# Two more up pairs in two by two form, and the first half's down rows added to x1 in DRAM

## The chip, the cores and the metric

The kernel runs on one core of one Trainium2 chip. The metric is the device time of one execution in microseconds (us). Before the change it is 693.52 us, the median of three runs (693.3 to 694.15). One further execution was taken with the hardware profiler; all rows quoted here come from it.

The engines are called as the profile calls them: PE (TensorE, matrix products; PEld is its loading of weights), DVE (VectorE), ACT (ScalarE), POOL (GpSimd) and SP (SyncE, which here only issues transfers). POOL also issues transfers, among them those that add to what already lies in DRAM.

## What is computed

A residual block for 512 tokens with 1024 channels: a normed input projection, a short convolution beside an attention, a gated merge, then a channel mixer. The change is in the channel mixer:

```python
h = rms_norm(x, norm_ffn_g[l])
up = causal_dwconv(h @ w_up[l], conv_ffn_w[l])
a, b = jnp.split(up, 2, axis=-1)
x = x + (jax.nn.silu(a) * b) @ w_down[l]
...
return rms_norm(x, norm_f_g)
```

`FFN_HIDDEN` is 2816, so `a` and `b` have 22 blocks of 128 channels each. The convolution has three taps along the tokens.

## The kernel before, in words

**Products in three parts.** Every matrix product is made of three in a rounded type: high part of the weights by high part of the data, low by high, high by low. So each weight tile that arrives (`raw_...`, on SP's queue, five buffers) is split by ACT into a high part (`wh_...`, line 267) and by DVE into a low part (`wl_...`, line 271). There are two buffers of each, so a split starts when PE has done with the tile two before.

**Two by two form.** Part of the products are computed on two by two blocks of quarters with seven products where eight would be usual. Such a product needs sums of weight quarters (made in DRAM ahead of time), sums of data quarters (made once by DVE), and sums of the results in PSUM (made by DVE). Weights in this form come as two chunks for each step: `P` (three plain quarters, from `wst`) and `F` (four sums, from `sums`).

**Sums of weights.** `todo` is a list of transfers, six for each group of weights: SP copies a part from `wst` (line 140), POOL adds another part onto it (line 143), and so on in turn, each waiting for the one before. One of the list is issued with each `tick()`, and `split()` ticks as the kernel goes along the stream of weights.

**The channel mixer's order.** Pairs j = 0 to 21 (one block of `a`, one of `b`) are made in two halves: pairs 0 to 11, then a pass over the down products with what they gave (`down`, 12 steps; its matmuls are `dn`), then pairs 12 to 21 and a second pass of 8 steps, and a plain rest and the last norm. In a plain pair each of the two blocks (`block`, matmuls `p_up`) takes 48 matmuls of 128 by 256; pairs 3 and 7 (`UPS`) are in two by two form (`up_pair`, matmuls `us`, then five sums on DVE, lines 1087 to 1092) with 84. They need the forms of x1 (sums of its quarters), which lie in the tile `xf`. After pair 7 the place of these forms is used again: its lower half takes x1 itself, reloaded from its copy `x1d` in DRAM by two transfers of POOL (line 1097), and its upper half is space for temporaries (`fz`).

**Behind each block** DVE multiplies with the norm's factor (`up`, line 1110), ACT and DVE apply the three taps (lines 603, 604, 607; output `fu`, three buffers), ACT applies silu to `a`, and POOL multiplies `a` by `b` (line 1123 for even pairs, 1130 for odd ones). For each two pairs DVE then forms quarter sums (lines 1140 to 1145), and ACT and DVE split the results into `gh` and `gl` (lines 1149, 1150), the data of the down products. Up to pair 7 the multiply works in place in PSUM, from pair 8 on it writes into `fz`.

**Down rows.** The output's first six row blocks are done as three rows i = 0, 1, 2 of two blocks in two by two form, the first half also row 3. The 8 PSUM banks are two sets, `X` and `Y`. When the products of a row are complete, `combine` puts seven sums on DVE and a copy on ACT into the list `later`, which `split()` works off beside the splits; they add the row to x1 in `xg`. Row 2 of the first half is `HELD`: its four banks (set Y) are not read out but stay open until the second pass goes on adding to them. So the second half's up blocks turn in the four banks of set X alone.

**One row read early.** For the end of the kernel, a piece of x1's last row is split into `gh` and `gl` (lines 1304, 1305). These need nothing but the reloaded x1.

Of the kernel before, what the change touches and what calls it, by code (L numbers as in the profile page):

```python
# [13 lines left out]
P = 128  # L14
D = 1024
S = 512
# [37 lines left out]
HELD = 2  # L54
GS = 2
NFF = len(STEPS[0]) + len(STEPS[1])
UPS = (3, 7)
# [7 lines left out]
def block_kernel(ctx, tc, xT, vecs, wv, win, wmix, wo, wup, wst, wdp, outT):  # L65
# [56 lines left out]
    ngate = len(groups)  # L122
    groups += [[NUP + 2 * j, NUP + 2 * j + 1] for j in range(len(UPS))]
    nup = len(groups)
    groups += [list(range(n, min(n + 2, NFF - 1))) for n in range(0, NFF - 1, 2)] + [[NFF - 1]]
# [28 lines left out]
    for i0, i1 in ((0, ngate), (ngate, len(groups))):  # L154
        for i in range(i0, i1, 4):
            todo += [op for ops in zip(*(group(x) for x in range(i, min(i + 4, i1)))) for op in ops]
# [83 lines left out]

    def split(hl=None):
# [6 lines left out]
        if k >= gs0 and (nm[0] in "imwu" or nm[0] == "F" and int(nm[1:]) % 2):  # L248
            tick()
            if nm[0] in "m":  # L250
                tick()
# [916 lines left out]
    def combine(ph, i, banks, ids):  # L1168

        m1, m2 = x1[:, 2 * i, :], x1[:, 2 * i + 1, :]  # L1170
        p23, p45, p16, p7 = banks[0], banks[1], banks[2], banks[3][:, th[0]]
        t = {}

        def z1():
            t["z"] = fz(f"cz{ph}{i}")
            nc.scalar.activation(t["z"][:, th[0]], p16[:, th[0]], AF.Copy)
            nc.vector.tensor_add(t["z"][:, th[1]], p16[:, th[1]], t["z"][:, th[0]])

        def a1():
            nc.vector.tensor_add(m1, p23, m1)  # L1180

        def u3():
            t["u"] = fz(f"cu{ph}{i}")[:, : 2 * P]
            nc.vector.tensor_add(t["u"], p7, t["z"][:, th[1]])
            nc.vector.tensor_add(m1[:, th[1]], p45[:, th[1]], m1[:, th[1]])

        def a2():
            nc.vector.tensor_sub(m2, m2, p45)

        def a3():  # L1190
            nc.vector.tensor_add(m1, m1, t["z"])

        def a4():
            m2h = m2.rearrange(halves_of, h=2)
            nc.vector.tensor_sub(m2h, m2h, t["u"].unsqueeze(1).to_broadcast([P, 2, 2 * P]))

        for f, us, x in ((z1, 0.42, 2), (a1, 0.7, 0), (u3, 0.85, 3), (a2, 0.7, 1), (a3, 0.7, None), (a4, 0.7, None)):
            later.append((0, us, () if x is None else ids if x == 3 else (ids[x],), f))
        if ph == 1:
            for m in (2 * i, 2 * i + 1):  # L1200
                later.append((0, 0.8, (), lambda m=m: final_square(m)))

# [18 lines left out]
    def down(ph, n0):  # L1221
# [13 lines left out]
        for n, (name, prods) in enumerate(todo):  # L1235
# [5 lines left out]
            for cs, i, g, b, h in prods:  # L1241
                if i not in open_:
# [235 lines left out]
```

## Time and profile before

| stage | from, us | to, us | PE busy | DVE busy | DMA share |
|---|---|---|---|---|---|
| projection, attention | 0.00 | 182.00 | 180.88 | 133.72 | 0.57, then 0.72 |
| gates and merge | 182.00 | 294.70 | 112.66 | 87.77 | 0.81 |
| output projection | 294.70 | 338.20 | 43.50 | 34.22 | 0.76 |
| pairs 0 to 11 | 338.20 | 466.60 | 128.40 | 111.98 | 0.71 |
| first down pass | 466.60 | 523.70 | 57.10 | 42.78 | 0.84 |
| pairs 12 to 21 | 523.70 | 632.50 | 108.80 | 77.95 | 0.51 |
| second down pass | 632.50 | 668.20 | 35.70 | 29.16 | 0.55 |
| rest and last norm | 668.20 | 691.40 | 17.26 | 16.48 | 0.26 |

The profiled execution itself took 693.39 us; its span, from the first to the last instruction, is 691.4 us. The table is read off windows of busy time: in a stage where PE's busy time is as long as the stage, PE had something to do throughout, and the time of the other engines lies beside it.

### The profile page before, as it was taken

What the parts mean: (1) busy time and instruction counts of PE and PEld (TensorE: products, weight loads), DVE (VectorE), ACT (ScalarE), POOL (GpSimd) and SP (SyncE); (2) the same over time, 40 slices, a digit from 0 to 9 for tenths busy, and PEclk for the clock granted to TensorE, in tenths of its full rate; (3) what the DMA queues carried; (4) which work ended last, traced back from release to release, by engine and by line L of the source; (5) the groups of instructions that cost most, each with busy time, mean ns of one, the idle gap of its engine ahead of it and who ended that gap; (6) DMA issues with size and microseconds to landing.
All of it is one profiled execution on the core that took longest, in us unless ns stands there. A gap on an engine that the chain in (4) does not pass through costs nothing.

```text
span 691.4 us, 14653 instructions
## 1 busy us (share of the span) xinstructions
PE 684.3 (99%) x5952; PEld 682.7 (99%) x5952; DVE 534.1 (77%) x844; ACT 359.0 (52%) x571; POOL 165.7 (24%) x192
## 2 busy tenths in 40 slices
PE   9999999999999999999999999999999999999996
PEld 9999999999999999999999999999999999999996
DVE  6678777886687777768887989978674678777786
ACT  6575556554564544446654535545443354444663
POOL 5123745444021010233311221340000211221000
PEclk9999999999999999999999999999999999999999
DMA  8526957578489796878686478579866374544623
GB/s 306 198 85 222 199 149 175 102 182 173 126 220 287 215 261 186 249 253 260 202 199 170 138 160 304 146 188 268 259 205 212 93 175 122 142 100 128 197 81 121
DMA packets 59202, 128.87 MB, mean 186 GB/s; under 512 B 5344, under 2 KB 26848, under 8 KB 58880
## 3 DMA queue, kind: packets, MB, share of 16 engines
q1 hardware_dynamic: 41280, 100.22, 44.8%
q0 software_dynamic: 17136, 27.04, 22.2%
q8 instruction: 46, 0.75, 0.4%
q10 hardware_dynamic: 720, 0.69, 0.3%
q14 instruction: 20, 0.16, 0.1%
HBM read 123.67 MB, written 41.42 MB: 239 GB/s over the span
## 4 chain that ended last, share of the span: by engine, by line
PE 96%; DVE 2%; ACT 1%; issue 1%; ACTq 0%; DVEq 0%
PE p_up L300 24%; PE p_in L300 14%; PE dn L318 13%; PE gs L318 8%; PE p_up L318 7%; PE p_wo L300 6%; PE yc L318 3%; PE ya L300 3%; PE us L318 3%; PE pa L512 2%; PE pb L514 2%; PE p_g L300 2%; PE o L693 2%; PE tp L678 1%; PE pdB L300 1%; PE pdA L300 1%
## 5 line engine op out<-in xcount | busy, mean ns | idle before, releaser
L300 PE MATMUL p_in<-xf,wh_in 128*128 128x256 f32 x576 | 95.7, 278 | 0.0
L300 PE MATMUL p_up<-x1h,wh_up 128*128 128x256 f32 x488 | 95.1, 276 | 0.0
L300 PE MATMUL p_up<-x1h,wl_up 128*128 128x256 f32 x488 | 95.1, 276 | 0.0
L300 PE MATMUL p_up<-x1l,wh_up 128*128 128x256 f32 x488 | 94.9, 276 | 0.0
L143 POOL DMA_DIRECT2D sum<-in_wst_dram x57 | 59.4, 1142 | 129.0 <-DMA sum<-sum 80.6
L300 PEld LDWEIGHTS p_in<-xf,wh_in 128*128 128x128 f32 x576 | 80.4, 188 | 0.7
L300 PEld LDWEIGHTS p_up<-x1h,wh_up 128*128 128x128 f32 x488 | 73.5, 188 | 0.0
L300 PEld LDWEIGHTS p_up<-x1h,wl_up 128*128 128x128 f32 x488 | 73.5, 188 | 0.0
L300 PEld LDWEIGHTS p_up<-x1l,wh_up 128*128 128x128 f32 x488 | 73.4, 188 | 0.0
L267 ACT ACTIVATE wh_up<-raw_up 128x1024 fp32r<-128x1024 f32 x40 | 42.3, 1057 | 52.0 <-PE p_up L300 47.3
L267 ACT ACTIVATE wh_F<-raw_F 128x1024 fp32r<-128x1024 f32 (+1 forms) x36 | 37.8, 1050 | 60.2 <-PE ya L300 25.9
L271 DVE TENSOR_TENSOR wl_F<-raw_F,wh_F 128x1024 fp32r<-128x1024 f32 (+1 forms) x36 | 44.4, 1232 | 21.8 <-ACT wh_F L267 21.5
L271 DVE TENSOR_TENSOR wl_up<-raw_up,wh_up 128x1024 fp32r<-128x1024 f32 x40 | 48.8, 1219 | 12.5 <-ACT wh_up L267 12.0
L300 PE MATMUL p_in<-xf,wl_in 128*128 128x256 f32 x288 | 56.5, 278 | 0.1
L1123 POOL TENSOR_TENSOR ge<-fu,fu 128x512 f32<-128x512 f32 x11 | 18.7, 1703 | 128.6 <-DVE fu L607 108.9
L267 ACT ACTIVATE wh_P<-raw_P 128x768 fp32r<-128x768 f32 (+1 forms) x36 | 30.0, 834 | 32.4 <-PE dn L318 15.0
L300 PEld LDWEIGHTS p_in<-xf,wl_in 128*128 128x128 f32 x288 | 43.5, 188 | 0.3 <-DVE wl_in L271 0.3
L271 DVE TENSOR_TENSOR wl_P<-raw_P,wh_P 128x768 fp32r<-128x768 f32 (+1 forms) x36 | 34.5, 957 | 9.8 <-PE gs L318 5.4
L318 PE MATMUL dn<-gl,wh_F 128*128 128x256 f32 x156 | 36.3, 276 | 0.0
L318 PE MATMUL dn<-gh,wh_F 128*128 128x256 f32 x156 | 36.3, 276 | 0.0
L318 PE MATMUL p_up<-x1h,wh_up 128*128 128x256 f32 x152 | 36.3, 276 | 0.0
L318 PE MATMUL p_up<-x1l,wh_up 128*128 128x256 f32 x152 | 36.3, 276 | 0.0
(353 smaller groups left out, 2012.4 us busy)
## 6 DMA issues: line engine op xcount, KB each, us to landing
raw_up<-in_wup_dram SPq DMA_DIRECT2D x40, 512.0 KB, 3.6
raw_F<-sum SPq DMA_DIRECT2D x35, 512.0 KB, 5.8
raw_P<-in_wst_dram SPq DMA_DIRECT2D x35, 384.0 KB, 4.3
raw_in<-in_win_dram SPq DMA_DIRECT2D x24, 512.0 KB, 3.6
sum<-in_wst_dram POOLq DMA_DIRECT2D x35, 256.0 KB, 5.6
sum<-in_wst_dram SPq DMA_DIRECT2D x17, 512.0 KB, 7.5
sum<-in_wst_dram POOLq DMA_DIRECT2D x17, 512.0 KB, 8.9
sum<-sum SPq DMA_DIRECT2D x34, 256.0 KB, 4.7
```

The source lines that it names most:

```text
L143: return lambda: keep(nc.gpsimd.dma_start(dst, src, accum_op=ALU.add))
L267: ins = nc.scalar.activation(hi, raw, AF.Copy)
L271: ins = nc.vector.tensor_sub(lo, raw, hi.bitcast(F32))
L300: keep(nc.tensor.matmul(out[:, cs], w, x[:, cs], start=start and i == 0 and c == 0, stop=stop and i == 2 and c == len(cut) - 1,))
L318: keep(nc.tensor.matmul(out, wl if x == 1 else wh, xl if x == 2 else xh, start=opens and bk not in seen, stop=closes and bk not in left,))
L512: keep(nc.tensor.matmul(pa[t][:, :VW], xt, w[:, :VW], start=start, stop=stop))
L514: keep(nc.tensor.matmul(pb[t], xt, w[:, VW:], start=start and t % 2 == 0, stop=stop and t % 2 == 1))
L678: keep(nc.tensor.transpose(tp[:, ks], pt[:, ks], ident))
L693: keep(nc.tensor.matmul(o[:, os_], vv[:, kb, pr, e, :], x[:, kb, cs], start=e == 0 and kb == 0 and i == 0, stop=e == 1 and kb == nk - 1 an ...
L1123: keep(nc.gpsimd.tensor_mul(ge, a.rearrange(halves_of, h=2), b.rearrange(halves_of, h=2)))
```

## The change

Pairs 13 and 17 become two by two pairs too. For that the forms of x1 stay in `xf` until pair 17, so the reload of x1 moves behind pair 17, and there is no x1 in the chip's memory when the first down pass ends. `combine` for the first half therefore builds the row alone, in tiles `cm`, and POOL adds it to `x1d` in DRAM. Row 2 is read out like the others, `HELD` goes, and the second half's up blocks turn in all eight banks. The multiply stays in PSUM up to pair 17. The list of weight sums gets two more groups, is put into another order, and `ticks` says how many transfers are issued with each split.

```diff
-HELD = 2
-UPS = (3, 7)
+UPS = (3, 7, 13, 17)
...
+    ends = [0, 4, len(groups)]
+    for (j0, j1), n0, n1 in zip(PHASES, (0, len(STEPS[0])), (len(STEPS[0]), NFF - 1)):
+        groups += [[NUP + 2 * i, NUP + 2 * i + 1] for i, j in enumerate(UPS) if j0 <= j < j1]
+        if j0:
+            ends.append(len(groups))
+        groups += [list(range(n, min(n + 2, n1))) for n in range(n0, n1, 2)]
+        if not j0:
+            ends += [ends[-1] + 4, len(groups)]
+    groups.append([NFF - 1])
+    ends += [len(groups) - 2, len(groups)]
...
+    def ticks(nm):
+        if nm[0] in "iw":
+            return 1
+        if nm[0] == "m":
+            return 2
+        if nm[0] == "u":
+            n = int(nm[2:])
+            return 2 if (n % 4 == 0 and n > 4) or (n >= 2 * PHASES[1][0] and n % 4 < 3) else 1
+        return int(nm[0] == "F" and (int(nm[1:]) % 2 == 1 or int(nm[1:]) >= NUP))
...
+        def tmp(name):
+            return fz(name) if ph else fp.tile([P, S], F32, tag="fu", name=name, bufs=3)
...
         def a1():
-            nc.vector.tensor_add(m1, p23, m1)
+            if ph:
+                t["m"] = [x1[:, m, :] for m in (2 * i, 2 * i + 1)]
+                nc.vector.tensor_add(t["m"][0], p23, t["m"][0])
+                return
+            combine.n += 1
+            if combine.n % 2:
+                m = [fp.tile([P, 2, 2 * P], F32, tag="ge", name=f"cm{i}{k}", bufs=2) for k in range(2)]
+            else:
+                g = fp.tile([P, 6, 2 * P], F32, tag="gr", name=f"cm{i}")
+                m = [g[:, 2 * k : 2 * k + 2, :] for k in range(2)]
+            t["m"] = [x.rearrange("p h c -> p (h c)") for x in m]
+            nc.vector.tensor_add(t["m"][0], p23, t["z"])
...
             nc.vector.tensor_add(m1[:, th[1]], p45[:, th[1]], m1[:, th[1]])
+            if not ph:
+                keep(nc.gpsimd.dma_start(x1d[:, 2 * i, :], m1, accum_op=ALU.add))
 
         def a2():
-            nc.vector.tensor_sub(m2, m2, p45)
+            m2 = t["m"][1]
+            if ph:
+                nc.vector.tensor_sub(m2, m2, p45)
+            else:
+                nc.vector.scalar_tensor_tensor(
+                    m2.rearrange(halves_of, h=2), p45.rearrange(halves_of, h=2), -1.0,
+                    t["u"].unsqueeze(1).to_broadcast([P, 2, 2 * P]), op0=ALU.mult, op1=ALU.subtract,
+                )
+                keep(nc.gpsimd.dma_start(x1d[:, 2 * i + 1, :], m2, accum_op=ALU.add))
...
+        for f, us, x in ops[: 6 if ph else 4]:
...
-                    (i, b) not in before and (ph, i) != (1, HELD), (i, b) not in after and (ph, i) != (0, HELD),
+                    (i, b) not in before, (i, b) not in after,
...
-                    if (i, 0) not in after and (ph, i) != (0, HELD):
+                    if (i, 0) not in after:
...
-            acc = ring(*X)
+            acc = ring(*X, *Y)
```

**Where the early read of x1 stands on ACT.** Before, at the end of the first down pass, among the splits (`wh`) of its last chunks and of blocks 24 and 25. What stands in brackets is whom an instruction waits for: DMAHW a transfer of SP, DMASW one of POOL, else an engine.

```order
L267 ACTIVATE wh_F_6856<-raw_F_6739 128x1024 [waits DMAHW4_49,DVE_49,PE_49]
L267 ACTIVATE wh_up_6887<-raw_up_6772 128x1024 [waits DMAHW5_49,DVE_49,PE_49]
L1304 ACTIVATE gh<-xg 128x256 [waits DMASW3_49,PE_49]
L267 ACTIVATE wh_up_6948<-raw_up_6798 128x1024 [waits DMAHW6_49,DVE_49,PE_49]
L1301 ACTIVATE gh<-ident 128x128 [waits PE_49]
```

Now, on the same engine, behind pair 17: `fu_7707` and `fu_7712` are pair 17's two blocks, `fu_7773` is block 36, `wh_up_7911` the split of block 39.

```order
L617 ACTIVATE fu_7712<-us_7570,vec 128x512 [waits DVE_49,Activation_49]
L617 ACTIVATE fu_7773<-xg,vec 128x512 [waits DVE_49]
L1345 ACTIVATE gh<-xg 128x256 [waits DMASW0_49]
L1134 ACTIVATE fu_7707<-fu_7707 128x512 [waits DVE_49,Activation_49]
L281 ACTIVATE wh_up_7911<-raw_up_7652 128x1024 [waits DMAHW5_49,PE_49]
L1134 ACTIVATE fu_7773<-fu_7773 128x512 [waits DVE_49,Activation_49]
L617 ACTIVATE fu_7835<-xg,vec 128x512 [waits DVE_49,Pool_49]
```

The copy from `xg` moved from the end of the first down pass to a place three taps behind pair 17, ahead of pair 17's silu (L1134) and block 39's split.

**POOL around the reload.** Before, behind pair 6's even product `ge`; `go_5659` is pair 7's product.

```order
L1123 TENSOR_TENSOR ge_5507<-fu_5437,fu_5502 128x512
L1097 DMA xg<-x1d 128x2048 x2
L1130 TENSOR_TENSOR go_5659<-fu_5645,fu_5650 128x512
L1123 TENSOR_TENSOR ge_5777<-fu_5711,fu_5772 128x512
L143 DMA sum_94<-in_wst_dram 256x1x256
```

Now, behind pair 16's; `go_7721` is pair 17's product, and the sums 103 and 104 are the last two groups of the second down pass.

```order
L1137 TENSOR_TENSOR ge_7567<-fu_7496,fu_7562 128x512
L148 DMA sum_103<-in_wst_dram 128x512
L148 DMA sum_104<-in_wst_dram 128x256
L1111 DMA xg<-x1d 128x2048 x2
L1144 TENSOR_TENSOR go_7721<-fu_7707,fu_7712 128x512
L148 DMA sum_103<-in_wst_dram 128x256
```

Two adds now stand between the even product and the reload.

**DVE behind the two by two pair that the reload follows.** Before, from the multiply of block 17 on (`p_up_5722`); `wl_up_5848` is the low part of block 19's weights.

```order
L1110 TENSOR_TENSOR xg<-p_up_5722,rb_n_4654 128x512
L1140 TENSOR_TENSOR go_5659<-ge_5507 128x256
L1141 TENSOR_TENSOR go_5659<-go_5659,ge_5507 128x256
L1144 SCALAR_TENSOR_TENSOR go_5659<-go_5659 128x256
L271 TENSOR_TENSOR wl_up_5848<-raw_up_5591,wh_up_5847 128x1024
L604 SCALAR_TENSOR_TENSOR fu_5772<-xg,vec,fu_5772 128x511
```

Now, from the multiply of block 37 on; `wl_up_7912` is the low part of block 39's weights.

```order
L1124 TENSOR_TENSOR xg<-p_up_7785,rb_n_4656 128x512
L1154 TENSOR_TENSOR go_7721<-ge_7567 128x256
L1155 TENSOR_TENSOR go_7721<-go_7721,ge_7567 128x256
L1158 SCALAR_TENSOR_TENSOR go_7721<-go_7721 128x256
L618 SCALAR_TENSOR_TENSOR fu_7835<-xg,vec,fu_7835 128x511
L1159 SCALAR_TENSOR_TENSOR go_7721<-go_7721 128x256
L621 SCALAR_TENSOR_TENSOR fu_7835<-xg,vec,fu_7835 128x510
L285 TENSOR_TENSOR wl_up_7912<-raw_up_7652,wh_up_7911 128x1024
```

The low part of the weights moved behind two taps and a quarter sum.

More of the change, by code (lines that the diff above doesn't have):

```diff
@@ L121, in block_kernel @@
     groups = [[NFF + 2 * j, NFF + 2 * j + 1] for j in range(KB - GS)]
[L122 to L125, printed above, removed]
+    ends = [0, 4, len(groups)]
[8 more added lines that the diff above has]
+    ends += [len(groups) - 2, len(groups)]
     nstep = [len(d) for d in STEPS[0] + STEPS[1]] + [2] * (2 * (KB - GS) + 2 * len(UPS))
@@ L152, in group @@
         ]
-    for i0, i1 in ((0, ngate), (ngate, len(groups))):
-        for i in range(i0, i1, 4):
-            todo += [op for ops in zip(*(group(x) for x in range(i, min(i + 4, i1)))) for op in ops]
+    for i0, i1 in zip(ends, ends[1:]):
+        todo += [op for ops in zip(*map(group, range(i0, i1))) for op in ops]
     def tick():
@@ L247, in split @@
         load(k + (LOOK if k >= gs0 else AHEAD))
-        if k >= gs0 and (nm[0] in "imwu" or nm[0] == "F" and int(nm[1:]) % 2):
-            tick()
-            if nm[0] in "m":
+        if k >= gs0:
+            for _ in range(ticks(nm)):
                 tick()
@@ L1168, in combine @@
     def combine(ph, i, banks, ids):
-        m1, m2 = x1[:, 2 * i, :], x1[:, 2 * i + 1, :]
         p23, p45, p16, p7 = banks[0], banks[1], banks[2], banks[3][:, th[0]]
         t = {}
+        def tmp(name):
+            return fz(name) if ph else fp.tile([P, S], F32, tag="fu", name=name, bufs=3)
         def z1():
-            t["z"] = fz(f"cz{ph}{i}")
+            t["z"] = tmp(f"cz{ph}{i}")
             nc.scalar.activation(t["z"][:, th[0]], p16[:, th[0]], AF.Copy)
@@ L1179, in a1 @@
         def a1():
-            nc.vector.tensor_add(m1, p23, m1)
+            if ph:
[10 more added lines that the diff above has]
+            nc.vector.tensor_add(t["m"][0], p23, t["z"])
         def u3():
-            t["u"] = fz(f"cu{ph}{i}")[:, : 2 * P]
+            t["u"] = tmp(f"cu{ph}{i}")[:, : 2 * P]
             nc.vector.tensor_add(t["u"], p7, t["z"][:, th[1]])
+            m1 = t["m"][0]
             nc.vector.tensor_add(m1[:, th[1]], p45[:, th[1]], m1[:, th[1]])
+            if not ph:
+                keep(nc.gpsimd.dma_start(x1d[:, 2 * i, :], m1, accum_op=ALU.add))
         def a2():
-            nc.vector.tensor_sub(m2, m2, p45)
+            m2 = t["m"][1]
[7 more added lines that the diff above has]
+                keep(nc.gpsimd.dma_start(x1d[:, 2 * i + 1, :], m2, accum_op=ALU.add))
         def a3():
-            nc.vector.tensor_add(m1, m1, t["z"])
+            nc.vector.tensor_add(t["m"][0], t["m"][0], t["z"])
         def a4():
-            m2h = m2.rearrange(halves_of, h=2)
+            m2h = t["m"][1].rearrange(halves_of, h=2)
             nc.vector.tensor_sub(m2h, m2h, t["u"].unsqueeze(1).to_broadcast([P, 2, 2 * P]))
-        for f, us, x in ((z1, 0.42, 2), (a1, 0.7, 0), (u3, 0.85, 3), (a2, 0.7, 1), (a3, 0.7, None), (a4, 0.7, None)):
+        ops = ((z1, 0.42, 2), (a1, 0.7, 0), (u3, 0.85, 3), (a2, 0.7, 1), (a3, 0.7, None), (a4, 0.7, None))
+        for f, us, x in ops[: 6 if ph else 4]:
             later.append((0, us, () if x is None else ids if x == 3 else (ids[x],), f))
@@ L1201, in combine @@
                 later.append((0, 0.8, (), lambda m=m: final_square(m)))
+    combine.n = 0
     def final_square(m):
```

## The prediction

> **What bounds the kernel now.** I read the page's first and fourth parts, then the chain of waits in order of time, then the windows of busy time by stage. Line numbers are those of before.
>
> ```profile
> span 691.4 us, 14653 instructions
> ...
> PE 684.3 (99%) x5952; PEld 682.7 (99%) x5952; DVE 534.1 (77%) x844; ACT 359.0 (52%) x571; POOL 165.7 (24%) x192
> ...
> PE 96%; DVE 2%; ACT 1%; issue 1%; ACTq 0%; DVEq 0%
> ```
>
> The chain runs through TensorE for 96% of the span; VectorE has it for 2%. A busy PE need not be a PE at its peak, so the chain is read in time:
>
> ```profile
> 371.40 9.52 PE us L318 x84
> 380.92 1.36 PE p_up L318 x12
> 382.28 4.08 PE p_up L300 x36
> ...
> 413.56 9.52 PE us L318 x84
> 423.08 1.36 PE p_up L318 x12
> ...
> 439.40 1.36 PE p_up L318 x12
> ...
> 466.60 57.12 PE dn L318 x504
> 523.72 1.36 PE p_up L318 x12
> ...
> 632.52 35.70 PE dn L318 x315
> ```
>
> Columns: start, length, what. Each piece begins where the last one ended (371.40 + 9.52 = 380.92), so there is no hole: matmuls follow each other every 1.36 / 12 = 0.1133 us. A plain up block is 12 + 36 matmuls and takes 5.44 us, a plain pair of two blocks 96 matmuls and 10.88 us; a two by two pair (3 and 7 so far, `us`) has 84 and takes 9.52 us. In this stretch a matmul less is 0.1133 us less, as long as nobody makes PE wait. So the question is what new waits come.
>
> **What goes.** Pairs 13 and 17 each change from 96 matmuls to 84: 2 x 12 x 0.1133 = **2.72 us** off PE. The down products stay the same in number; only their start and stop flags change for row 2, which is no longer kept open.
>
> **What is added to the other engines, and what covers it.** First VectorE, the busiest of them:
>
> ```profile
> 381.00:413.50 32.50, 32.50 (x289) 32.50 (x288) 29.79 (x46) 13.65 (x21) 8.80 (x7) 1.00 0.62 146
> ...
> 524.00:578.00 54.00, 54.00 (x479) 54.00 (x478) 36.73 (x51) 21.27 (x30) 9.38 (x8) 1.00 0.54 149
> 578.00:632.50 54.50, 54.50 (x484) 54.50 (x483) 41.17 (x59) 25.12 (x36) 12.85 (x11) 1.00 0.48 121
> ```
>
> Columns: stretch, its length, busy time of PE, PEld, DVE, ACT, POOL, granted clock, DMA share, GB/s. In the second half's ups DVE works 36.73 + 41.17 = 77.9 of 108.5 us. Prices of what comes:
>
> ```profile
> L271 DVE TENSOR_TENSOR wl_F<-raw_F,wh_F 128x1024 fp32r<-128x1024 f32 x2 | 2.4, 1220 | 0.9 <-ACT wh_F L267 0.9
> L271 DVE TENSOR_TENSOR wl_P<-raw_P,wh_P 128x768 fp32r<-128x768 f32 x2 | 1.9, 948 | 0.0
> ...
> L271 DVE TENSOR_TENSOR wl_up<-raw_up,wh_up 128x1024 fp32r<-128x1024 f32 x1 | 1.2, 1226 | 1.0 <-ACT wh_up L267 1.0
> ...
> L1090 DVE TENSOR_TENSOR us<-us,uz 128x512 f32<-128x512 f32 x1 | 0.7, 700 | 0.0
> ...
> L1180 DVE TENSOR_TENSOR xg<-dn,xg 128x512 f32<-128x512 f32 x3 | 2.1, 689 | 2.4 <-PE dn L318 2.4
> ...
> L1184 DVE TENSOR_TENSOR xg<-dn,xg 128x256 f32<-128x256 f32 x3 | 1.2, 416 | 0.0
> ```
>
> A pair in two by two form splits four chunks (2 x 0.95 + 2 x 1.22 = 4.34 us) where two blocks took 2 x 1.22 = 2.44, and has five sums (three of 256 columns at 0.42, two of 512 at 0.70 = 2.66): 4.56 us more, 9.1 for both. Closing row 2 at the end of the first down pass adds two sums of 512 and three of 256 columns, 2.6 us, at the head of this stage. DVE then has 77.9 + 9.1 + 2.6 = 89.6 us in 108.5 - 2.7 = 105.8, 85%. The first row above is the stage with pairs 4 to 6 of the first half: 29.79 of 32.50, 92%, and PE full. So DVE's sum is hidden. In the first down pass the three other rows lose two of seven operations each; nothing is late there. The step kept in PSUM (multiply and taps of pairs 8 to 17 now read a PSUM bank in place) I price at nothing: eight banks turn where the second half had four, and the next user of a bank comes 9.5 us later or more, but for the second down pass, whose last bank (block 43's) is first written over 2 us after that block ends, against 0.69 us for its multiply.
>
> **The wait that is new.** The reload of x1 moves from behind pair 7 to behind pair 17, and with it come two instructions that read its last row, ACT's `gh<-xg` and DVE's `gl<-xg`; before, they stood at the end of the first down pass, long after the reload. ACT's copy now stands behind the tap of block 36, ahead of pair 17's silu and the split of block 39. Nobody has timed pair 17, but pair 7 is its twin, with the same operations on PE, ACT, DVE and POOL, so I lay the copy into pair 7's rows:
>
> ```profile
> L1097 POOL DMA_DIRECT2D xg<-x1d x2: 552/590/627, 423.4 to 424.0; - x2
> ...
> DMA to landing us min/median/max: 8.0/9.4/10.8
> ```
> ```profile
> 430.56 0.72 ACT L603 ACTIVATE fu<-xg,vec 128x512 f32<-128x512 f32 x1
> 432.11 0.63 ACT L1120 ACTIVATE fu<-fu 128x512 f32<-128x512 f32 x1 [0.83 <-DVE fu L607]
> 434.00 1.07 ACT L267 ACTIVATE wh_up<-raw_up 128x1024 fp32r<-128x1024 f32 x1 [1.25 <-PE p_up L300]
> ...
> 435.85 0.72 ACT L603 ACTIVATE fu<-xg,vec 128x512 f32<-128x512 f32 x1 [0.27 <-POOL go L1130]
> ```
> ```profile
> 434.17 1.64 POOL L1130 TENSOR_TENSOR go<-fu,fu 128x512 f32<-128x512 f32 x1 [9.62 <-DVE fu L607]
> ```
> ```profile
> 436.69 1.21 DVE L271 TENSOR_TENSOR wl_up<-raw_up,wh_up 128x1024 fp32r<-128x1024 f32 x1
> 437.82 0.74 DVE L604 SCALAR_TENSOR_TENSOR fu<-xg,vec,fu 128x511 f32<-128x511 f32 x1
> 438.49 0.41 DVE L1145 SCALAR_TENSOR_TENSOR go<-go 128x256 f32<-128x256 f32 x1
> 438.82 0.74 DVE L607 SCALAR_TENSOR_TENSOR fu<-xg,vec,fu 128x510 f32<-128x510 f32 x1
> ```
>
> The second half of the reload, which holds the row read, was issued at 424.0 and took 10.8: landed at 434.8. ACT would reach the copy at 431.3 (430.56 + 0.72) and stand until 434.8. Behind it in line: the silu (0.63), POOL's product of pair 17 that needs it (1.64), ACT's tap that needs the product's buffer (0.72), then on DVE one tap, one sum, one tap and the low half of block 39's weights, which the changed order puts after these three (0.66 + 0.34 + 0.66 from start to start, 1.21). With the copy itself (0.3, an estimate: 256 columns against the silu's 512) and 0.2 for hand-overs that is 6.4 us from landing to weights. PE wants them at block 39's ninth matmul, 439.40 + 8 x 0.1133 = 440.3, so a landing up to 433.9 costs nothing, and each us behind that stops PE for one. At 434.8 it is **0.9 us**. The ends: nothing if the reload lands 0.9 us sooner; more if later. No further wait follows: behind block 39's weights DVE has six operations (0.6 from start to start) and the split of block 40 (1.21), 4.8 us, and a block lasts 5.44.
>
> Does it land sooner? While it ran the DMA engines were full:
>
> ```profile
> 423.00:434.60 11.60, 11.60 (x105) 11.60 (x104) 11.53 (x19) 4.92 (x8) 1.60 (x3) 1.00 1.01 398
> ```
>
> At 398 GB/s, 4.6 MB, of which the reload is 2.1. At pair 17, SP's copies for the sums are smaller, and two weight loads start later, since SP stands in line for an add; but two adds (256 and 128 KB) go out on POOL's queue just ahead of the reload. These about cancel; I take 0.5 us, between nothing and 0.9. The Trainium skill, "DMA: Bandwidth & Descriptors", section "Anatomy of one DMA — SWDGE (gpsimd) path", fits such a transfer as about 2.0 us plus its bytes at 436 GB/s, by which I estimate 4.4 us for each of these two. The trace disagrees with 8.0 and 10.8, under full DMA engines; by the page the landing would cost nothing.
>
> **The queues that the new steps pass.** The sums of pairs 13 and 17 are built before the first down pass, so SP waits for POOL's adds ahead of that pass's loads:
>
> ```profile
> 450.14 1.30 POOL L1130 TENSOR_TENSOR go<-fu,fu 128x512 f32<-128x512 f32 x1 [5.76 <-DVE fu L607]
> ```
> ```profile
> sum<-in_wst_dram POOLq DMA_DIRECT2D x17, 512.0 KB, 8.9
> ...
> raw_P<-in_wst_dram SPq DMA_DIRECT2D x35, 384.0 KB, 4.3
> ```
>
> Pair 17's first add stands behind pair 9's product: issued at 451.4, landed 8.9 later, at 460.3. SP's next copy waits for it, and behind that the load of the second P chunk, now at about 461, in at 465.5. PE wants it at 466.60 + 4.76 = 471.4, less ACT's 0.84 for the split: 5 us to spare. The eight adds into x1 are issued from POOL after the rows close; their readers are the reload, 100 us later, and the next writer of the same buffer. Priced at nothing.
>
> **Sum.** The profiled execution took 693.39 us, 2.0 more than its span, and the median of the runs is 693.52, 0.13 above. 693.39 - 2.72 + 0.5 = **691.2**.
>
> **Rivals.** Two of them need rows: DVE's split of the second plain block behind pair 3, and POOL's even product ahead of the reload with the landing of its adds.
>
> ```profile
> 395.83 1.21 DVE L271 TENSOR_TENSOR wl_up<-raw_up,wh_up 128x1024 fp32r<-128x1024 f32 x1
> ```
> ```profile
> 418.80 2.14 POOL L1123 TENSOR_TENSOR ge<-fu,fu 128x512 f32<-128x512 f32 x1 [8.44 <-DVE fu L607]
> ```
> ```profile
> sum<-in_wst_dram POOLq DMA_DIRECT2D x35, 256.0 KB, 5.6
> ...
> sum<-in_wst_dram POOLq DMA_DIRECT2D x3, 128.0 KB, 6.6
> ```
>
> - No new wait: the reload lands by 433.9 of pair 7's clock. For it: fewer bytes on SP's queue. Against it: the twin's 434.8. 693.39 - 2.72 = 690.7. By the fit of the Trainium skill's page named above, this would be the outcome.
> - DVE's backlog at pair 13 is not hidden. Behind pair 3 this split ended at 397.0; its block began at 380.92 + 3 x 5.44 = 397.2 and wanted it at 398.1, so 1.1 us were to spare. If the 2.6 us of row 2 shift it whole, PE stops 1.5 us: 692.2, and 692.7 with the reload. Against it: those 2.6 us fall at the head of pair 12, where DVE has free time (36.73 busy of 54.00).
> - SP's line: pair 17's first add or the loads behind it take over 5 us longer than their rows, and the first down pass stops for about 2 us: 692.7. The add of 512 KB would have to take 14 us.
> - Slower: POOL's queue runs in line, the reload moving only once the two adds ahead of it have landed. By the twin's clock they go out between the even product's end (420.9) and the reload (423.4); the second lands 6.6 later, from 427.5 to 430.0, in the middle 428.7. The reload then moves 5.3 us later and lands at 440.1: 6.2 us of PE, 696.9. From a landing past 433.9 + 2.72 + 1.39 = 438.0 on, the kernel is slower. Against it: in the twin two halves of the reload were under way at once, 0.6 us apart at the start and landing 3.4 apart.
>
> **How the numbers follow.** Forecast 691.2 (own range 690.7 to 691.7): 0.45. No wait 0.22, DVE 0.14, SP 0.09, slower 0.10. A difference under 0.2% (1.39 us: 692.0 to 694.8) can hardly be measured. Faster: the first two, a third of DVE's and of SP's cases, 0.75; same: the rest of those and 0.02 of the last, 0.17; slower 0.08. The range goes from 690.4 (0.3 under the lowest case, since the three runs of before lie 0.85 apart) to 692.8, and leaves out the last case and some of SP's.
>
> **What would show it.** In the chain of the changed kernel: two more `us` pieces of 9.52 us; no hole at pair 13; a hole of 0 to 1 us in block 39, behind the first eight matmuls, released by `wl_up`; ACT's `gh<-xg` idle for some us, put down to the reload; `dn` unbroken from its start. The prediction is wrong if PE stops anywhere else for over 1 us, or if the reload's landing is past 11 us.

## The result: 1.24 us less, where 2.3 had been forecast

The changed kernel takes 692.03 us (median of 18 runs, 691.67 to 692.52), the kernel before 693.27 (18 runs, 693.09 to 694.15): a ratio of 0.998, 95% interval 0.9973 to 0.9988. The forecast of 691.2 was 0.8 too low; the range 690.4 to 692.8 holds the time. The interval leaves out 1, so the change does make the kernel faster, but by 0.18%, just under the 0.2% below which the prediction called a difference hardly measurable. Four single executions of later sessions were slow ones (707 and 859 us of the kernel before, over 2,400 of `e6_before_dve16` and of `e15_best`) and no comparison below rests on them. The profiled execution took 691.91 us, with a span of 690.1. All line numbers from here on are those of the changed kernel, unless said otherwise.

The page of the changed kernel, its first part:

```profile
span 690.1 us, 14688 instructions
...
PE 681.7 (99%) x5928; PEld 679.9 (99%) x5928; DVE 542.5 (79%) x857; ACT 362.2 (52%) x578; POOL 182.3 (26%) x206
```

PE has 24 matmuls and 2.6 us less. The chain of waits of the changed kernel in order of time, from the first down pass on (start, length, what):

```profile
466.68 57.12 PE dn L332 x504
...
534.68 9.52 PE us L332 x84
...
576.84 9.57 PE us L332 x84
586.40 1.36 PE p_up L332 x12
...
602.72 1.36 PE p_up L332 x12
...
629.92 35.70 PE dn L332 x315
```

Pairs 13 and 17 are there as pieces of 9.52 and 9.57 us, block 39 (602.72) is whole, and the second down pass starts at 629.92. Before the change it started at 632.52: **2.60 us earlier**, which is, but for rounding, 2.72 less the 0.08 by which PE is later at the first down pass already (466.60 became 466.68) and 0.05 in pair 17. So on PE the whole saving arrived, and no hole came. It is kept up to the last multiply of DVE, before the change

```profile
685.50 2.48 DVE L1340 TENSOR_TENSOR xg<-xg,pb_n 128x512 f32<-128x512 f32 x4 [0.80 <-PE pb_n L380]
```

and after it

```profile
682.90 2.48 DVE L1381 TENSOR_TENSOR xg<-xg,pb_n 128x512 f32<-128x512 f32 x4 [0.80 <-PE pb_n L394]
```

These end at 687.98 and 685.38, again 2.60 apart. But from there to the end of the span it is 691.37 - 687.98 = 3.39 us before the change and 690.11 - 685.38 = 4.73 after it. **The tail behind the last computation grew by 1.34 us**; 2.60 - 1.34 is the 1.26 by which the spans differ. In that tail only the last piece of the output goes out and SP waits for it. SP's waits in the last stretch, before the change (engine, line, whom it waited for, us, times, longest):

```profile
SPq L1473 <- DMA out_dram<-xg: 2.1, 4, 0.6
```

and after it:

```profile
SPq L1514 <- DMA out_dram<-xg: 3.4, 1, 3.4
```

Before, SP passed its final row of semaphores as one output after another landed; now it stands at the first of them until all have landed. The window of the transfers from the last multiply's end to the end of the span, in 40 slices, shows what landed late. Before the change (688.1 to 691.4, slices of 0.083 us):

```profile
DMA  9999999999999999999995000000000000000000
GB/s 385 385 385 385 385 385 372 397 397 397 397 372 385 348 373 385 385 385 397 385 397 162 13 0 0 0 0 0 0 0 0 0 0 0 0 0 0 0 0 0
```

After it (685.5 to 690.1, slices of 0.115 us):

```profile
DMA  9999999999999994010000000000000000000000
GB/s 383 410 365 365 410 365 383 392 419 392 365 392 338 365 374 134 27 18 9 9 18 18 27 27 0 0 0 0 0 0 0 0 0 0 0 0 0 0 0 0
...
q14 instruction: 1, 0.01, 1.1%
```

Before, all 16 DMA engines end together. After, at 687.3 fifteen of them are done, and something goes on for 0.9 us at about 18 GB/s, which is about what one engine of sixteen moves (385 / 16 = 24). And in this window lies one read of instructions (queue q14), which the window before the change doesn't have: 8 KB, begun at 1.24 us behind the last multiply and 0.78 us long. So I read: a piece of some engine's program is fetched while the last output goes out, one DMA engine carries it, and its share of the output comes late.

### The profile page after: what moved, and what is told of

Read it like the earlier page. It is cut to its first block, busy times and chain, and to the rows that moved or that the text cites. A ratio compares the mean times of both kernels' runs of the same rounds, so it can differ in the third digit from the quotient of the medians.

```text
span 690.1 us, 14688 instructions
## 1 busy us (share of the span) xinstructions
PE 681.7 (99%) x5928; PEld 679.9 (99%) x5928; DVE 542.5 (79%) x857; ACT 362.2 (52%) x578; POOL 182.3 (26%) x206
## 4 chain that ended last, share of the span: by engine, by line
PE 95%; DVE 2%; ACT 1%; issue 1%; ACTq 0%; DVEq 0%
PE p_up L314 22%; PE p_in L314 14%; PE dn L332 13%; PE gs L332 8%; PE p_up L332 7%; PE p_wo L314 6%; PE us L332 6%; PE yc L332 3%; PE ya L314 3%; PE pa L526 2%; PE pb L528 2%; PE p_g L314 2%; PE o L707 2%; PE tp L692 1%; PE pdB L314 1%; PE pdA L314 1%
## 5 line engine op out<-in xcount | busy, mean ns | idle before, releaser
L148 POOL DMA_DIRECT2D sum<-in_wst_dram x63 | 66.0, 1180 | 112.4 <-DMA sum<-sum 83.5
L314 PE MATMUL p_up<-x1h,wl_up 128*128 128x256 f32 x440 | 85.7, 276 | 0.0
L314 PE MATMUL p_up<-x1l,wh_up 128*128 128x256 f32 x440 | 85.7, 276 | 0.0
L314 PE MATMUL p_up<-x1h,wh_up 128*128 128x256 f32 x440 | 85.7, 276 | 0.0
L285 DVE TENSOR_TENSOR wl_F<-raw_F,wh_F 128x1024 fp32r<-128x1024 f32 (+1 forms) x40 | 50.2, 1256 | 27.8 <-ACT wh_F L281 26.6
L314 PEld LDWEIGHTS p_up<-x1h,wl_up 128*128 128x128 f32 x440 | 66.3, 188 | 0.0
L314 PEld LDWEIGHTS p_up<-x1l,wh_up 128*128 128x128 f32 x440 | 66.2, 188 | 0.0
L314 PEld LDWEIGHTS p_up<-x1h,wh_up 128*128 128x128 f32 x440 | 66.2, 188 | 0.0
L281 ACT ACTIVATE wh_up<-raw_up 128x1024 fp32r<-128x1024 f32 x36 | 38.0, 1055 | 25.5 <-PE p_up L314 16.6
L285 DVE TENSOR_TENSOR wl_in<-raw_in,wh_in 128x1024 fp32r<-128x1024 f32 x24 | 30.2, 1256 | 6.1 <-ACT wh_in L281 6.0
L332 PE MATMUL p_up<-x1h,wh_up 128*128 128x256 f32 x136 | 32.5, 276 | 0.0
```

The lines of the kernel that those rows point to most:

```text
L148: return lambda: keep(nc.gpsimd.dma_start(dst, src, accum_op=ALU.add))
L281: ins = nc.scalar.activation(hi, raw, AF.Copy)
L285: ins = nc.vector.tensor_sub(lo, raw, hi.bitcast(F32))
L314: keep(nc.tensor.matmul(out[:, cs], w, x[:, cs], start=start and i == 0 and c == 0, stop=stop and i == 2 and c == len(cut) - 1,))
L332: keep(nc.tensor.matmul(out, wl if x == 1 else wh, xl if x == 2 else xh, start=opens and bk not in seen, stop=closes and bk not in left,))
```

## The experiments

The theories on the tail: **A**, the fetch belongs to DVE's program, which the change made 16 instructions longer (1,074 to 1,090 in the trace); **B**, it belongs to SP's, made 20 longer (443 to 463); **C**, the fetch is harmless, and the order in which SP passes its final semaphores costs the time. (ACT's and POOL's programs grew as well, by 17 and 27 instructions; the runs that lengthen DVE's alone decide on those too.) That order has its own part: SP waits for its eight transfer semaphores in a fixed order, 0.06 us each. Before the change the last output signals the seventh of them, after it the first, since SP issues ten more transfers; so seven rows remain when the last output has landed, not one.

This table has what the profiled execution of each kernel shows, in us. "Landing" is the time from the issue of the last output to its last write, "rows" the time from there to SP's last wait, "tail" the time from the last multiply's end to the end of the span. The median is of all runs of that kernel; the profiled execution can lie off it (`e2_sp6` 691.88, `e5_both` 692.17, `e7_rest` 698.61, `e11_best` 693.06).

| kernel | median | last multiply ends | landing | rows | tail |
|---|---|---|---|---|---|
| before | 693.27 | 687.98 | 1.91 | 0.47 | 3.39 |
| changed | 692.03 | 685.38 | 2.83 | 0.90 | 4.73 |
| e1_sp8 | 692.27 | 685.27 | 2.86 | 1.28 | 5.14 |
| e2_sp6 | 691.54 | 685.85 | 2.64 | 0.63 | 4.26 |
| e3_dve24 | 705.39 | 701.32 | 2.25 | 0.80 | 4.07 |
| e4_before_dve16 | 710.48 | 704.24 | 2.90 | 0.53 | 4.43 |
| e5_both | 691.16 | 686.84 | 1.92 | 0.43 | 3.35 |
| e6_before_dve16 | 693.97 | 688.04 | 2.66 | 0.44 | 4.10 |
| e7_rest | 695.74 | 693.08 | 1.91 | 0.50 | 3.42 |
| e10_late | 698.88 | 692.28 | 2.84 | 0.89 | 4.73 |
| e11_best | 691.92 | 687.94 | 1.91 | 0.43 | 3.34 |
| e12_rest | 693.95 | 688.45 | 1.91 | 0.48 | 3.50 |
| e13_only13 | 693.28 | 687.99 | 1.91 | 0.62 | 3.53 |
| e15_best | 690.85 | 685.30 | 1.91 | 0.43 | 3.34 |

### The tail: whose code, and which semaphore

Runs `e1_sp8` and `e2_sp6`, with n = 8 and 6:

```diff
+    for i in range(n):
+        keep(nc.sync.dma_start(pad[:, i, :], vecs[i : i + 1, :P]))
     warm_to = bank(5, "warm_to")[:, : 2 * P]
```

> The changed kernel with eight tiny transfers (512 bytes each, DRAM to DRAM) added on SP's queue in its idle time between the last weight load and the outputs. Eight keeps the outputs on the same completion semaphores and makes SP's own program nine instructions longer; DVE's program is the same. The tail (from the end of the last DVE multiply to the end of the span) was 3.4 us before the change and 4.7 us after. Theory A (an 8 KB piece of DVE's code is read just then and holds up one DMA engine in the last output by 0.9 us): the tail stays at 4.7, time 692.0 (691.8 to 692.3). Theory B (the same, but it is SP's code): the read moves ahead of the last output, the tail falls by 0.9 to 3.8, time 691.1. Theory C (only the order in which SP passes its final semaphores matters): tail 4.7, time 692.0.

> As the run above, but six tiny transfers: the last output then signals the seventh of SP's eight completion semaphores, as before the change, not the first. SP passes these in a fixed order at the end, 0.06 us each. Theory A (DVE's code read) with the order of the semaphores: one row of wait is left behind the last landing in place of seven, so the tail falls by about 0.4 to 4.3, time 691.6. Theory B (SP's code read) with the order: tail 3.4, time 690.7. Rival (the order costs nothing): no different from the run with eight.

Measured: with eight, 692.27 us (692.17 to 694.14), landing 2.86, so SP's program being longer moved nothing, and B falls. The tail was 0.4 longer than any theory gave: SP stood 0.37 us between two of its final rows, for which I have no cause. With six, 691.54 (691.4 to 691.88), a median 0.49 under the changed kernel's, the landing still late (2.64) and the rows 0.27 shorter: the order of the semaphores has a price of some tenths, and C alone does not do, since the landing is late in both.

Runs `e3_dve24` (on the changed kernel, n = 24) and `e4_before_dve16` (on the kernel before, n = 16):

```diff
     nc.vector.memset(ones, 1.0)
+    pad = cp.tile([1, n], F32, tag="pad", name="pad")
+    for i in range(n):
+        nc.vector.memset(pad[:, i : i + 1], 0.0)
```

> The changed kernel with 24 memsets of one element added at the head of DVE's program, where DVE waits for the first loads; SP's program and the semaphores of the outputs are the same. Theory A (DVE's code read stands in the last output): the read comes 24 instructions earlier in the program, the last output lands 1.9 us after its issue in place of 2.8, the tail falls by 0.9 to 3.8 and the time to 691.1 (up to 0.5 more if the memsets themselves delay the start). Theory B (SP's code) and theory C (order only): the tail stays 4.7, time 692.0 or a little over.

> The kernel before the change with 16 memsets of one element at the head of DVE's program, which gives DVE's program the length that it has after the change. Theory A: an 8 KB code read now appears in the last output of the kernel before as well, whose last output lands about 0.9 us later; the tail grows from 3.4 to 4.3, time 694.2 (693.9 to 694.7). Theories B and C: tail 3.4, time 693.3 plus at most 0.5 for the memsets at the start.

Of the tail, both came as theory A says, though not all of the lateness went. In `e3_dve24` no fetch lies in the tail and the output lands after 2.25; in `e4_before_dve16` the kernel before has a fetch in its tail and a landing of 2.90. That 2.25 is not 1.91 has another reason: in `e3_dve24` all DMA engines are slower and end together (701.4 to 704.0, slices of 0.065 us),

```profile
DMA  9989999798999999898998988989989862000000
```

and in `e4_before_dve16` too the DMA engines that the fetch leaves alone end some 2.2 us behind the issue. So these two runs show whose fetch it is, and the next two what it costs. In each of five traces this fetch begins when 1,086 or 1,087 of DVE's instructions have begun (in the traces of the changed kernel and of these four), whatever SP's count is (435 to 462); with 24 more ahead of it, it begins 14.2 us before the last multiply ends, not 1.2 behind it. The later runs agree: it stands at 1,086 or 1,087 again (at 1,095 in `e11_best`, in the middle of its memsets), and the kernels whose DVE program ends before that (`e7_rest`, `e12_rest` and `e13_only13`, with 1,074, 1,074 and 1,083) have no read in the tail and land after 1.91.

The times were far off, by 13 and 17 us, and the reason isn't the one that I wrote into the expectation of the next runs: on every engine the order of the instructions is the same but for the memsets, no scheduler moved anything. Matmuls became slower. Chain of `e3_dve24`, the pieces of pair 13, pair 17 and the second down pass:

```profile
546.17 9.86 PE us L335 x84
...
590.32 9.86 PE us L335 x84
...
645.90 35.71 PE dn L335 x315
```

84 matmuls in 9.86 us and not 9.52, without a hole and at full clock, while the down pass runs as before. The gates' two by two pieces (`gs`, 84 matmuls) are slower as well, 9.92 for 9.52. The runs below put as many memsets elsewhere and stay at 9.52. They differ in two things: when the memsets run, and where their tile lies, here among the constants, ahead of later tiles, whose places it can shift. That the places matter is my guess; it was not tried.

So as many memsets were put late: a tile of the pool `fp`, memsets in DVE's free time. Runs `e5_both` and `e6_before_dve16`; the second edit is in `e5_both` alone:

```diff
+    pad = fp.tile([1, n], F32, tag="pad", name="pad")
+    for i in range(n):
+        keep(nc.vector.memset(pad[:, i : i + 1], 0.0))
     warm_to = bank(5, "warm_to")[:, : 2 * P]
...
-        for g in range(4):
+        for g in range(2 + 2 * t):
+            n = 4 - 2 * t
             keep((nc.sync, nc.scalar)[t * (g % 2)].dma_start(
-                outT[:, 2 * g : 2 * g + 2, hs], x1[:, 2 * g : 2 * g + 2, hs]
+                outT[:, n * g : n * g + n, hs], x1[:, n * g : n * g + n, hs]
```

> The changed kernel with both causes of the longer tail taken away: 24 memsets of one element in DVE's program during the last down rows (every other instruction of PE, DVE, ACT and POOL stands where it stood), so that DVE's code read falls earlier, and the first half of the output sent in two transfers and not four, so that the last output signals the seventh of SP's eight final semaphores, as before the change. If code read and order of the semaphores are the whole of the 1.3 us: last output lands 1.9 to 2.3 us after its issue, tail 3.4 to 3.8, time 690.7 to 691.1, and this beats both kernels. If the tail has another cause: 692.0.

> The kernel before the change with 16 memsets of one element in DVE's program, set where they leave the order of all other instructions as it was (the run with memsets at the head had let the scheduler reorder the program). DVE's program then has the length that it has after the change. Code read: it falls into the last output, which lands 2.8 to 2.9 us after its issue in place of 1.9; tail 4.3 in place of 3.4; time 694.2 (693.9 to 694.5). Otherwise: 693.3.

`e6_before_dve16` took 693.97 beside 693.25 for the kernel before: 16 memsets in DVE's free time cost 0.7 us, all of it in the tail (4.10 for 3.39). Its window behind the last multiply (688.1 to 692.1, slices of 0.1 us) has the one engine's rest and the fetch:

```profile
GB/s 389 389 369 399 369 379 389 389 369 410 369 441 369 358 348 379 348 348 123 0 31 20 20 31 20 31 10 0 0 0 0 0 0 0 0 0 0 0 0 0
...
q14 instruction: 1, 0.01, 1.3%
```

`e5_both` has the tail of before, 3.35 us with a landing of 1.92. Theory A with the order of the semaphores accounts for the 1.34 us: 0.92 for the landing and 0.43 for the rows. Its time was 691.16 (690.68 to 692.17), just above its forecast of 690.7 to 691.1, and its six runs fall apart: four from 690.7 to 691.3, two at 692.1 and 692.2. The profiled one is the last of these, and shows where the time goes.

### The new wait for the reload, after all

ACT in the changed kernel and in `e5_both` (start, length, line, what, in brackets the idle time before and whom it waited for). Changed:

```profile
596.88 0.42 ACT L1345 ACTIVATE gh<-xg 128x256 fp32r<-128x256 f32 x1 [1.97 <-DMA xg<-x1d]
```

`e5_both`:

```profile
598.24 0.42 ACT L1345 ACTIVATE gh<-xg 128x256 fp32r<-128x256 f32 x1 [3.24 <-DMA xg<-x1d]
```

PE in `e5_both`, the eighth and ninth matmul of block 39 and the next:

```profile
603.50 0.28 PE L332 MATMUL p_up<-x1l,wh_up 128*128 128x256 f32 x1
604.34 0.74 PE L332 MATMUL p_up<-x1h,wl_up 128*128 128x256 f32 x4 [0.56 <-DVE wl_up L285]
```

The transfers of the reload, changed kernel (POOL issues two, the landing is counted from the issue):

```profile
L1111 POOL DMA_DIRECT2D xg<-x1d x2: 560/582/605, 586.7 to 587.3; - x2
...
DMA to landing us min/median/max: 7.4/8.5/9.5
```

In the changed kernel's profiled execution the half that holds the row landed after 9.5 us, at 596.8, and the copy ran at 596.88. In `e5_both` it took 10.8, as in the twin before the change, and PE stopped 0.84 - 0.11 = 0.73 us where the prediction said, released by `wl_up`; a second stop of 0.33 follows 6 us later. With slower matmuls right behind the stops, the second down pass starts 1.46 later than in the changed kernel (631.38 for 629.92). Two runs with the same order of ACT, DVE, POOL and PE lie between: in `e1_sp8` the copy ran at 597.08, and PE did not stop; in `e2_sp6` it ran at 597.58, and the first twelve matmuls of block 39 took 0.28 longer than 1.36:

```profile
602.86 1.64 PE p_up L334 x12
```

So the wait is real, the cover ends half a microsecond behind 596.9, and in these four profiled executions the landing decides whether it is paid.

Run `e10_late` delays the reload on purpose:

```diff
+            keep(nc.gpsimd.dma_start(pdr, x1d[:, 0:4, :]))
             for a in range(0, KB, 4):
                 nc.gpsimd.dma_start(x1[:, a : a + 4, :], x1d[:, a : a + 4, :])
```

> The changed kernel with one more transfer of 1 MB (x1 in DRAM to a scratch place in DRAM) on POOL's queue just ahead of the reload of x1. Reading of the trace: the low half of block 39's weights was ready 0.3 us before PE asked for it, so the wait for the reload was hidden with 0.3 us to spare, and each us by which the reload lands later stops PE for one, behind the first eight matmuls of block 39. At the 335 GB/s of that stretch 1 MB takes 3.1 us: reload lands 3 to 4 us later, PE stops 2.7 to 3.7 us, time 694.7 to 695.7. Rival (ACT's copy has a wider cover, and the wait of 0.5 us in the prediction was never near): PE stops less than the delay by over 1 us, time under 694.

The reload landed 14.0 us after its issue, the copy ran at 601.55, 4.67 us later, and PE stopped 0.72 + 3.10 + 0.26 = 4.1 us in and around block 39. The rival falls: past the cover, each microsecond of landing is one of PE (the transfer of 1 MB delayed the reload by 4.5 us, not by the 3 to 4 expected). But the kernel lost 6.9 us (698.88, last multiply at 692.28). The windows say where the other 2.8 went (columns as in the prediction: after the five engines come granted clock, DMA share, GB/s):

```profile
590.00:602.60 12.60, 12.60 (x114) 12.60 (x113) 9.33 (x15) 3.87 (x7) 0.00 (x0) 1.00 0.94 351
...
606.40:613.20 6.80, 5.57 (x26) 5.58 (x27) 6.80 (x9) 2.00 (x3) 2.90 (x2) 0.50 0.37 108
613.20:620.00 6.80, 6.80 (x62) 6.80 (x61) 4.83 (x8) 2.31 (x3) 0.78 (x1) 1.00 0.64 202
```

During the stop the granted clock fell to half (from 606.4 on), and stayed there for 6.8 us. The Trainium skill, "TensorE: Matmul & The Clock Gate", section "Part 1: The HAM clock gate (the "warmup" mystery)", has it that the clock is halved after an idle window of about 3.4 us and restored after a busy one. The trace agrees with the length, 6.8 us being two such windows, but not with the condition: in the 3.4 us before the fall PE ran eight matmuls (603.5 to 604.5), so less than a whole window without work was enough here. The stops of `e5_both` (0.73 and 0.33 us) left its clock at 0.999 over the span.

### The rest of the change, and pair 13 alone

Run `e7_rest` has `UPS = (3, 7)`, with reload, closed rows and products in PSUM as changed; pairs 13 and 17 are plain pairs again, 96 matmuls each. `e12_rest` is the same with two orders held. The edit of both (the lines of the reload move into a function `reload`):

```diff
-UPS = (3, 7, 13, 17)
+UPS = (3, 7)
...
+        if j == 17:
+            reload()
...
-            z = p if j <= UPS[-1] else fz(f"fz{j}{s_}")
+            z = p if j <= 17 else fz(f"fz{j}{s_}")
```

and in `e12_rest` and `e13_only13` (`UPS = (3, 7, 13)`) also

```diff
-            nc.gpsimd.dma_start(x1[:, a : a + 4, :], x1d[:, a : a + 4, :])
+            keep(nc.gpsimd.dma_start(x1[:, a : a + 4, :], x1d[:, a : a + 4, :]))
...
-    nc.scalar.activation(xlast[0], y7, AF.Copy)
+    with after_split():
+        nc.scalar.activation(xlast[0], y7, AF.Copy)
```

> The changed kernel without its two pairs: pairs 13 and 17 in three products as before (96 matmuls each), but with all the rest of the change (reload of x1 at pair 17, first half's rows closed and added in DRAM, products in PSUM, the new order of SP's and POOL's transfers). If the rest is free on the path of PE: no hole in PE, the last DVE operation ends where it does before the change (688.0, give or take 0.15), DVE's program is as long as before, so tail 3.4 and time 693.3. Rival, that the rest costs or saves something that the two pairs hid: the last DVE operation ends more than 0.3 us from 688.0, and a hole shows where.

> The changed kernel without its two pairs, again, but with the reload of x1 held to its place at pair 17 and ACT's early copy held back to the end (in the first such run the scheduler moved the reload into the first down pass and the copy to 545.6 us, where ACT stood 9.1 us behind it, PE stopped 3.4 us and its clock fell to half). If the rest of the change is free: no hole in PE after 210 us, last DVE operation at 688.0 give or take 0.15, tail 3.4, time 693.3 (693.1 to 693.5). If it is not: a hole that neither pair can have caused.

> As the run above, with pair 13 in two by two form and pair 17 still in three products. Twelve matmuls less, 1.36 us: last DVE operation at 686.6. DVE's program is 9 instructions longer than before the change and so still too short for the code read in the last output; that output signals the fourth of SP's eight final semaphores, four rows of 0.06 us behind it in place of one: tail 3.6. Time 692.1 (691.8 to 692.4). If pair 13 stops PE through DVE's backlog (a rival on record, up to 1.5 us): a hole near 545 us, time 693 or more.

`e7_rest` missed: 695.74. The reload was issued at 509.8 and 537.5, ACT's copy stood ahead of the splits and waited 9.1 us for it, PE stopped 1.5 and 1.7 us between 545 and 550 and ran 3.4 us at half clock. It is the same wait in another place, and says nothing of the rest.

`e12_rest` took 693.95, 0.6 over its forecast. Up to the second down pass it is as forecast: no hole, and the pass starts at 632.57, where it starts before the change (632.52). So the rest is free up to there, but for ACT's copy, whose wait this run leaves out. What it lost comes behind the down passes: with the copy held back to the last steps, its low half on DVE (0.34 us at 675.9) stands among the last sums, ACT reaches its squares of the last rows at 677.8 and not 676.5, and PE has a gap of 0.4 us at 679.1 that neither kernel has. `e13_only13` took 693.28, 1.2 over. It has no hole near 545, and the up blocks end at 631.42 where those of `e12_rest` end at 632.57; its stage starts 0.20 later, so pair 13 is worth its 1.36. But PE has the same gap of 0.4 us near the end, and the second down pass stops for 0.5 us at its start, with this chain:

```profile
627.33 4.09 PE p_up L314 x36
631.42 0.02 issue
631.44 0.70 DVE xg L1128
632.15 0.04 issue
632.19 0.86 PE dn L332 x5
```

With one pair less in the ring of eight banks, the last block's bank falls to an early row of the pass, which must wait for DVE's multiply. In the changed kernel, with both pairs, it doesn't: the prediction's remark that this bank is first written 2 us later holds for that rotation alone.

### A version that beats both

`e11_best` is `e5_both` with the copy held back as in `e12_rest`; `e15_best` puts copy and memsets into the second down pass (the copy's old lines go, and the output goes out as in `e5_both`):

```diff
                 with after_split():
                     nc.scalar.activation(ex[:, NT + 1 :], eps, AF.Sqrt)
+                    y7 = x1[:, KB - 1, halves[1]]
+                    nc.scalar.activation(gh[:, 41, :], y7, AF.Copy)
+                    nc.vector.tensor_sub(gl[:, 41, :], y7, gh.bitcast(F32)[:, 41, :])
+                    pad = fp.tile([1, 24], F32, tag="pad", name="pad")
+                    for i in range(24):
+                        nc.vector.memset(pad[:, i : i + 1], 0.0)
```

> The run with both causes of the longer tail taken away, and ACT's early copy out of x1 (the operation that stood behind the reload) put behind the last weight split, some 80 us later, where the reload has long landed. If the stop of PE in block 39, seen in the profiled execution of the run before this one (reload 1.3 us later, PE 1.1 us), comes only through that copy: no hole in PE after 210 us, last DVE operation ends at 685.4, tail 3.3 to 3.5, time 690.7 (690.5 to 690.9) in nearly all executions, and no longer some at 692. If the late landing reaches PE by another way: times spread to 692 as before, a hole after 600 us.

> The changed kernel with three edits: ACT's early copy out of x1 (with DVE's low half of it) put into the second down pass, 50 us after the reload; the 24 memsets of one element right behind it, where DVE has free time; the first half of the output in two transfers. The last such run had the copy and the memsets among the last sums, where they held the last steps up by about 1 us; here nothing of the last steps moves. If reload, code read and order of the semaphores are all that the change's saving was lost to: no hole in PE after 210 us, last DVE operation at 685.4, tail 3.4, time 690.7 (690.5 to 690.9) in nearly all executions. If something else costs: time near 692 again, and the profile shows where.

`e11_best` took 691.92, 1.2 over its forecast: no hole in block 39, the tail 3.34, but copy and memsets stood among the last sums and made a hole of 0.9 us at 678. (Its profiled execution, 693.06, also reaches the first down pass 1.6 us late.) `e15_best` took **690.85 us**, ratio 0.9964 (0.9953 to 0.9975) to the kernel before; the changed kernel's, of another session, is 0.998. Five of its runs lie within the forecast's 690.5 to 690.9, others at 690.2, 691.1 and 692.9. Its reload landed after 10.2 us, later than in the changed kernel, and PE has no hole (this landing, at 597.4, lies at the edge of the old cover, so the trace alone would not show that a late one is free; what shows it is that no instruction of the up stage waits for it any more):

```profile
576.77 9.55 PE us L332 x84
...
602.64 1.36 PE p_up L332 x12
...
629.84 35.70 PE dn L332 x315
```

Its transfers behind the last multiply (685.4 to 688.6, slices of 0.08 us) end together, as before the change, and no instruction read lies among them:

```profile
DMA  9999999999999999999999500000000000000000
GB/s 410 384 384 371 359 372 410 384 397 397 358 397 371 372 372 410 384 397 371 384 384 371 167 13 0 0 0 0 0 0 0 0 0 0 0 0 0 0 0 0
```

## Why the prediction was right, and where it was not

- **2.72 us off PE: right.** Two pieces of 9.52 and 9.57 us; the up stage as a whole is 2.60 shorter at its end, and `e13_only13` shows 1.36 for one pair.
- **DVE's sum hidden: right.** 89.6 us of 105.8 had been forecast for the second half's ups; the row shows 90.66 of 106.10, with PE full:

```profile
523.80:629.90 106.10, 106.10 (x938) 106.10 (x938) 90.66 (x129) 50.61 (x74) 32.05 (x27) 1.00 0.77 213
```

  No hole at pair 13: the rival of DVE's backlog is out.
- **SP's line: no wait.** The first down pass is one piece of 57.12 us. The eight adds into DRAM and the products in PSUM, priced at nothing, are free too, as `e12_rest` shows up to 632.57.
- **The new wait, 0.5 us: mechanism right, size off.** The step laid the copy into the twin's clock and said that a landing up to 433.9 costs nothing, one at 434.8 costs 0.9. Block 39 starts 163.32 later than the twin's (602.72 for 439.40), so the limit is 597.2 there; from landing to weights 6.4 us had been forecast, and `e5_both` and `e10_late` took 6.1, which puts it at 597.5. The changed kernel's profiled execution landed at 596.8 and paid nothing, so on PE it came as the rival "no new wait" has it; `e2_sp6` landed at 597.5, right at the limit, and paid 0.3; `e5_both` landed at 598.2, paid 0.73 at block 39 and was 1.46 late in the end. What I took for one number between two ends is a wait that comes in some executions and not in others. How often the changed kernel pays it is not shown, since one execution of it was traced. That no further wait follows was wrong: in `e5_both` DVE needed 5.9 us from block 39's weights to block 40's (604.28 to 610.19), not 4.8, and PE stopped again for 0.33. By the fit that the prediction took from the Trainium skill, "DMA: Bandwidth & Descriptors", section "Anatomy of one DMA — SWDGE (gpsimd) path", an estimated 4.4 us for a half, the wait could never come. The traces disagree: under full DMA engines the two halves took 7.4 and 9.5 us in the changed kernel, 8.6 and 10.8 in `e5_both`.
- **POOL's queue in line: out.** The reload landed 9.5 us after its issue; the rival had it at 16 (424.0 to 440.1 in the twin's clock). Its price was right in kind: `e10_late` pays it, and the halved clock on top, which the prediction had not counted.
- **The step that failed is the last one, the sum.** It carried the profiled execution's own end over unchanged ("2.0 more than its span") and took for granted, without saying so, that what lies behind the last multiply stays as it is. That term was 0 and measured 1.34 us: 0.92 for a fetch of DVE's code in the last output, 0.43 for the order of SP's semaphores. With it and the 0.12 by which PE's saving fell short of 2.72, 693.39 - 2.72 + 0.12 + 1.34 = 692.1, beside 692.03; without it and the wait, 690.7, beside 690.85 for `e15_best`.
- **That the range holds the time is in part luck.** The forecast's own range, 690.7 to 691.7, misses 692.03 by 0.3. Two terms were wrong in opposite directions, the wait (0.5, measured 0 in the traced execution) and the tail (0, measured 1.34). The upper part of the wide range had been drawn for DVE's backlog and SP's line, neither of which came; the tail was among none of the rivals.

## What to carry to other kernels

When an edit lengthens an engine's program or changes how many transfers are issued, the tail behind the last computation can move with no instruction of it changed: compare the last multiply's end to the end of the span in both traces before explaining a saving that came out short. A wait whose cover is within half a microsecond of a transfer's landing is not a small cost but a chance; move the reader to a place where it can't matter, as `e15_best` does. And where stops of PE add up to some 3 us within a few microseconds, count the halved clock behind them.

## What the hardware showed that was not expected

- An engine's program is read in pieces of 8 KB while it runs, over the same DMA engines as the data. For DVE that is one about every 128 instructions: in the trace of the kernel before, such reads stand where 320, 449, 577, 706, 832 and 959 of its instructions have begun, and the next would be due at 1,087, past its 1,074. In the last output such a read cost 0.7 to 0.9 us; what the others cost was not measured.
- With a tile of 24 (or 16) floats among the constants, the matmuls of the up blocks and of the gates' two by two pieces ran 3.6 to 4.8% slower (9.86 to 9.98 us for 84, not 9.52), with the order of all other instructions unchanged, while those of the down passes kept their pace; the last output landed later too (2.25 us without a fetch, not 1.91). The cause is open.
- Stops of 0.7 and 3.1 us, with eight matmuls between them, put PE at half clock for 6.8 us in `e10_late`; in `e7_rest` 3.4 us at half clock followed stops of 1.5 and 1.7 us, again with eight matmuls between. The stops of 0.73 and 0.33 us in `e5_both` did not touch it.
